# One decoder layer on one core: the last mLSTM head's second split in another buffer, value tiles in another order of PSUM banks, and the right-side loads of the cross-attention queries held behind another load

## The chip, the cores and the metric

The kernel runs on one core of one Trainium2 chip. The metric is the device time of one execution in microseconds (us), lower is better. The program uses the five engines of the core: PE (matrix multiply), DVE (vector), ACT (activation functions and scaled copies), POOL (GpSimd) and SP, which here issues all the DMAs. Each engine runs its own queue of instructions in order.

## The reference, cut to what matters

The layer works on `SEQ = 1024` tokens of width 1024 and 256 memory tokens, all in float32.

```python
h = rmsnorm(x, ln1[l]); z = h @ w_in[l]
mh = mlstm_chunkwise(mq, mk, mv, ig, lf)              # 4 heads of 128
mh = mh * lax.rsqrt(jnp.mean(mh * mh, axis=-1, keepdims=True) + EPS)
ml_out = (mh * ml_norm).reshape(B, S, ML_W) * jax.nn.sigmoid(ml_o)
fx_out = forgetting_attention(fq, fk, fv, flf)        # 8 heads of 64
x = x + jnp.concatenate([ml_out, fx_out], axis=-1) @ w_out[l]
x = x + cross_attention(rmsnorm(x, ln_x[l]), rmsnorm(mem, ln_mem[l]), w_xq[l], w_xkv[l], w_xo[l])
u = jax.nn.relu(rmsnorm(x, ln2[l]) @ w_ff1[l])
x = x + (u * u) @ w_ff2[l]
return rmsnorm(x, ln_f)
```

## The kernel before, in words

Activations are kept with the features on the 128 partitions and the tokens along the free dimension, in two halves of 512 tokens (`hf` 0 and 1). Nearly every product is made of three matmuls on a value that is cut into a high and a low part (`mm3`, L186 to L188): low weight by high input, high by low, high by high. `split` makes the two parts: one ACT copy for the high part (L134, or L137 with a scale) and one DVE subtraction for the low part (L135 or L138).

The stages that the change touches, in order of time:

- **mLSTM head, closing part** (`ml_head`, L568 to L633). For each half it loads a row of factors `fb` into the buffer `r_a` (one buffer; L253 for the first half, L625 for the second), multiplies the head's output by norm and gate (DVE L628, L629), splits it (ACT L137, DVE L138) and stores the parts to the DRAM tensor `mix` (L632, L633). The high part `yh` stands in `r_y`, of which there is one buffer; the low part stays in `r_f`. `r_d` has two buffers.
- **Values of the forgetting attention** (`token_major(a["w_fv"], fv_sink, ...)`, L1092). Sixteen tiles of 24 matmuls (128x256 outputs). Each tile takes a PSUM bank from `mm()`, which goes round the list `banks`: "mm", "tp", "m2", "tp" (the profile calls m2 "m"). "tp" has two banks, "mm" and "m2" one each. Tile 0 takes "mm" and tile 15 "tp": 64 tiles have been drawn since the count `turn` was last set to 0. `fv_sink` splits each tile (ACT L137, DVE L138 with `rcol`) into `r_b`, `r_p` or `r_c` in turn and stores it. The planner mixes these matmuls with the first 13 slots of the attention.
- **Slots of the forgetting attention** (`slot`, L1026). One slot has one score part (`sc` banks, PE L734 and L735), its maximum (DVE L741 or L744), its exponential (ACT L756) and, from the 14th slot on, one value step: transposes into a "tp" bank (PE L782), a split into `r_d` and `r_e` (ACT L134, DVE L135; every third step uses a `w4` buffer), and the product (PE L801). Inside the slots the order of each compute engine is fixed by hand (`in_order`).
- **Second part of the output projection** (`full_sink`, L1122 to L1134). Sixteen tiles, in the order half 0 features 0 to 3, half 1 features 0 to 3, half 0 features 4 to 7, half 1 features 4 to 7. Each loads a piece of `x1d` (L1125), adds it (DVE L1126), stores it back (L1127), and adds its square to a sum (ACT L222, POOL L226). `mix_done` keeps the store of half 1, feature 5, the 14th of the sixteen.
- **Queries of the cross-attention.** `query_whole(hd)` makes the queries of half 0 for one of four heads as plain products: two weight loads from `w_xq` (L174, two `wr` buffers), two products, one in "mm" and one in "m2" (one bank each), each split into `r_b` and `r_c`, or `r_p` and `r_a` or `r_y`. `right_side(hd)` (L1168 to L1188) prepares, for the queries of half 1, which are made by a seven-product scheme, one quarter of the right sides: it loads two pieces of `x1d` into the two `r_f` buffers, here called x (feature `hd`) and y (feature 4 + `hd`) (L1176), scales each (ACT L1177), and makes sums and differences on POOL (`sub`, L1339), each split into an "act" buffer. In code order: cut 11 (from x), cut 21 and 22 (from y), difference and cut t1 (from x alone), difference and cut t2 (t1 and y), difference and cut t3 (x and y), a last difference. The loop calls `query_whole(hd)`, `right_side(hd)` and `cross_head(hd, 0, ...)` for the four heads; the last loads keys and values (L1276, L1277).

What sets the order outside the slots is a planner (`schedule_with_timeline_sim`): it plays the program through with modelled durations, and gives each engine, SP too, the instructions in the order in which they become ready there, earlier code first. Data dependencies and free buffers are waited for. `tc.issue_after(i)` adds that the loads in its body stand behind instruction i in the queue that issues them; it waits for no completion.

Of the kernel before, what the change touches and what calls it, by code (L numbers as in the profile page):

```python
# [10 lines left out]
F32R = mybir.dt.float32r  # L11
# [6 lines left out]
P = 128  # L18
# [5 lines left out]
MLH = 4  # L24
# [20 lines left out]
def hybrid_layer(ctx: ExitStack, tc: tile.TileContext, a: dict, out: bass.AP):  # L45
# [9 lines left out]
    def name(tag):  # L55
        count[0] += 1
        return f"{tag}_{count[0]}"

    def sb(tag, shape, bufs, dt=F32):
        return pool.tile(shape, dt, tag=tag, name=name(tag), bufs=bufs)  # L60
# [18 lines left out]
    def w2(tag, n=512, dt=F32, p=P):  # L79
        return sb("r_" + tag, [P, 512], BUFS[tag], dt)[:p, :n]  # L80
# [6 lines left out]
    def ps_tile(tag):  # L87
        return psum.tile([P, 512], F32, tag=tag, name=name(tag), bufs=PBUFS[tag])

    def sc():  # L90
        return ps_tile("sc")
# [4 lines left out]
    def ov_():  # L96
        return ps_tile("ov")

    turn = [0]
    banks = ["mm", "tp", "m2", "tp"]  # L100
# [10 lines left out]
    load = nc.sync.dma_start  # L111
# [57 lines left out]
    def weights(src, n=1024):  # L169
        return weight_parts(weight_load(src, n))  # L170

    def weight_load(src, n=1024):
        raw = sb("wr", [P, 1024], 2)[:, :n]
        load(raw, src)  # L174
        return raw

    def weight_parts(raw):
        n = raw.shape[1]
        hi = sb("wh", [P, 1024], 3, F32R)[:, :n]
        lo = sb("wl", [P, 1024], 3, F32R)[:, :n]  # L180
        split(hi, lo, raw)
        return hi, lo
# [7 lines left out]
    def both(pair, f):  # L190
        return f(pair[0]), f(pair[1])
# [66 lines left out]
    def proj(w, x, tiles, kn=KT, order=None, into=None):  # L258

        wv = both(w, lambda t: t.rearrange("p (k c) -> p k c", k=kn))  # L260
        for half, n in order or [(hf, n) for n in range(tiles) for hf in range(2)]:
            ps = mm() if into is None else into
            for k in range(kn):
                mm3(ps, both(wv, lambda t: t[:, k, n * P : (n + 1) * P]), both(x[half], lambda t: t[:, k]), k == 0, k == kn - 1)
            yield n, half, ps
# [163 lines left out]
    ps = ov_()  # L429
# [58 lines left out]
    def token_major(w_src, sink, cs=(0, 1), between={}):  # L488

        for c in cs:  # L490
            ws = [both(weights(w_src[c, i]), lambda t: t.rearrange("p (k c) -> p k c", k=4)) for i in range(2)]
            for t in range(8):
                if t in between:
                    between[t]()
                hf, tt = divmod(t, 4)
                ps = mm()[:, 0:256]
                for k in range(KT):
                    x = both(h[hf], lambda z: z[:, k, tt * P : (tt + 1) * P])
                    mm3(ps, x, both(ws[k // 4], lambda z: z[:, k % 4]), k == 0, k == KT - 1)
                sink(t, c, ps)  # L500
# [67 lines left out]
    def ml_head(hd, q, k, og, num1, den1):  # L568
        fac = col("fac", 8)
        nums = []  # L570
        dens = col("dens", 8)
        sqs = col("sqs", 8)
        for hf in range(2):
            nmb = w2("a")
            load(nmb, rows[hd : hd + 1, hf * TH : hf * TH + TH].broadcast_to([P, TH]))
            num = ov_()
            acc = den1 if hf else w2("b")
            last = 4 * hf + 3
            for j in range(4 * hf, last + 1):
                d0 = j - 4 * hf  # L580
                c0 = min(d0 * P, 256)
                sp = sc()
                ks = both(k, lambda z: z[:, j * P : (j + 1) * P])
                mm3(sp[:, c0:], ks, both(q, lambda z: z[:, hf * TH + c0 : hf * TH + TH]), True, True)
                wt = acc if j == 0 else w2("c")
                s.activation(wt[:, c0:], nmb[:, c0:], AF.Exp, bias=gcol[:, j, hd : hd + 1])
                n_ = d0 * P + P - c0
                g.affine_select(out=wt[:, c0 : c0 + n_], in_=wt[:, c0 : c0 + n_], pattern=[[1, n_]], compare_op=ALU.is_ge, fill=0.0, base=c0 - d0 * P, channel_multiplier=-1)
                v.scalar_tensor_tensor(out=wt[:, c0:], in0=sp[:, c0:], scalar=float(P) ** -0.5, in1=wt[:, c0:], op0=ALU.mult, op1=ALU.mult)
                wh, wl = w2("d", dt=F32R), w2("e", dt=F32R)  # L590
                split(wh[:, c0:], wl[:, c0:], wt[:, c0:])
                if j:
                    g.tensor_tensor(out=acc[:, c0:], in0=wt[:, c0:], in1=acc[:, c0:], op=ALU.add)
                vj = mv_of(hd, j)
                mm3(num[:, c0:], (vj[:, :P], vj[:, P:]), (wh[:, c0:], wl[:, c0:]), d0 == 0, j == last)
            sq = w2("c")
            if hf:
                nsb = num1
                v.tensor_tensor(out=nsb, in0=num, in1=nsb, op=ALU.add)
                s.activation(sq, nsb, AF.Square)  # L600
            else:
                nsb = w2("f")
                s.activation(nsb, num, AF.Copy)
                s.activation(sq, num, AF.Square)
            ps = sc()
            sum_cols(ps[:, 0:4], acc, 4)
            sum_cols(ps[:, 4:8], sq, 4)
            s.activation(dens[:, 4 * hf : 4 * hf + 4], ps[:, 0:4], AF.Abs)
            v.tensor_copy(sqs[:, 4 * hf : 4 * hf + 4], ps[:, 4:8])
            nums.append(nsb)  # L610
        v.tensor_tensor(out=dens, in0=dens, in1=emc[:, :, hd], op=ALU.max)
        rd = col("rd", 8)
        v.reciprocal(rd, dens)
        v.tensor_tensor(out=sqs, in0=sqs, in1=rd, op=ALU.mult)
        v.tensor_tensor(out=sqs, in0=sqs, in1=rd, op=ALU.mult)
        rsqrt_cols(fac, sqs, 1.0 / P, 8)
        v.tensor_tensor(out=fac, in0=fac, in1=rd, op=ALU.mult)
        yield
        for hf in range(2):
            fb = w2("a")  # L620
            at = facd[hd : hd + 1]
            if hf == 0:
                to_row(fb, fac, 8, at, sc)
            else:
                load(fb, at[:, TH:].broadcast_to([P, TH]))  # L625
            yield
            y = nums[hf]
            v.scalar_tensor_tensor(out=y, in0=y, scalar=vec[:, VEC["ml_norm"] + hd : VEC["ml_norm"] + hd + 1], in1=fb, op0=ALU.mult, op1=ALU.mult)  # L628
            v.scalar_tensor_tensor(out=y, in0=og[:, hf * TH : hf * TH + TH], scalar=1.0, in1=y, op0=ALU.add, op1=ALU.mult)  # L629
            yh, yl = w2("y", dt=F32R), y.bitcast(F32R)  # L630
            split(yh, yl, y, 0.5)
            load(mix[hf, 0, :, hd], yh.bitcast(F32))  # L632
            load(mix[hf, 1, :, hd], yl.bitcast(F32))  # L633
# [454 lines left out]
    for i in range(LEAD_):  # L1088
        slot(False, 0)
        if i in (1, 11):  # L1090
            next(closing, None)
    token_major(a["w_fv"], fv_sink, between={4: lambda: next(closing, None)})  # L1092
    hm = act().rearrange("p a b -> p (a b)").rearrange("p (e k c) -> p e k c", e=2, k=KT)
    load(hm.bitcast(F32), hmd)
# [20 lines left out]
    h2 = act(), act()  # L1115
    x1_accs = [w2("b"), w2("b")]
    mix_done = []
# [21 lines left out]
    for n0 in (0, 4):  # L1139
        ws = [weights(a["w_out_b"][n0 // 2 + i], 6 * P) for i in range(2)]  # L1140
        for hf in range(2):
            for n in range(n0, n0 + 4):
                w = both(ws[n // 2 % 2], lambda t: t.rearrange("p (k c) -> p k c", k=3)[:, :, n % 2 * P : n % 2 * P + P])
                ps = mm()
# [23 lines left out]
    def right_side(k):  # L1168
        if not fourth:
            for c in (("11", "21"), ("t1", "t2"), ("22", "t3")):  # L1170
                right_room(*c)
            fourth.append(w4((P, 4, 256)))
        x, y = w2("f"), w2("f")
        for t, n in ((x, k), (y, 4 + k)):
            with tc.issue_after(mix_done[0].ins):
                load(t, x1d[1, :, n])  # L1176
            s.activation(t, t, AF.Copy, scale=ln_x(n))  # L1177
        x1, x2, y1, y2 = (t[:, e * 256 : e * 256 + 256] for t in (x, y) for e in range(2))
        cut_right("11", k, x1)
        cut_right("21", k, y1)  # L1180
        cut_right("22", k, y2)
        sub(x1, x2, x1, g)
        cut_right("t1", k, x1)
        sub(x1, y2, x1, g)
        cut_right("t2", k, x1)
        sub(x2, y2, x2, g)
        cut_right("t3", k, x2)
        sub(fourth[0][:, k], y1, x1, g)  # L1188

    def q_room(kk):  # L1190
        return [rotate(*tags).bitcast(F32R) for tags in ((("b",), ("c",)), (("p",), ("a", "y")))[kk]]

    def query_whole(hd):
        q = []
        for kk in range(2):
            t = q_room(kk)
            for _, _, ps in proj(weights(a["w_xq"][2 * hd + kk]), [h2], 1, order=[(0, 0)], into=ps_tile(("mm", "m2")[kk])):
                split(*t, ps, 1.0 / 16.0)
            q.append(t)
        return q  # L1200
# [488 lines left out]
    for at, (b, m) in enumerate(steps):  # L1689
# [16 lines left out]
        for i, of, y, op in ((1, 1, x22, ALU.add), (5, 5, x22, ALU.add), (7, 7, x22, ALU.add), (6, 6, x22, ALU.add), (2, 1, x11, ALU.add), (4, 5, x21, ALU.subtract), (3, 7, x12, ALU.subtract)):  # L1706
            if of == i:
                held[of] = bank()
            ps = held[of]
# [138 lines left out]
```

## Time and profile before

| | us |
|---|---|
| median of 3 runs | 1512.09 (1512.07 to 1512.88) |
| the profiled execution's own time | 1510.96 |
| its span, first to last instruction | 1509.2 |
| PE busy in the span | 1493.0 (99%) |
| DVE, ACT, POOL busy | 1122.7, 757.7, 528.7 |
| mean granted PE clock | 0.997 |

The profiled execution's own time is 1.76 us above its span and 1.13 us below the median. With PE busy for 99% of the span, what can be won or lost without changing the matmuls is the idle time of PE and the time in which its clock is lower. A profile line names an instruction group by source line, engine, operation and tiles (`r_f<-x1d` is a load of `x1d` into an `r_f` buffer).

### The profile page before, as it was taken

Reading aid. Unit: us, or ns where it says so; the run is one execution under the profiler, and the core shown is the slowest. Engines: PE = TensorE matmul, PEld = TensorE weight load, DVE = VectorE, ACT = ScalarE, POOL = GpSimd, SP = SyncE. Lnnn points to the kernel's source line nnn. Section 1 sums busy time; section 2 is a strip of 40 time slices with the busy share of each in tenths; the row PEclk is TensorE's granted clock in tenths of the full one; section 3 lists DMA queues with packets and bytes.
Section 4 is the critical chain, followed back from the end, with each engine's and each line's share of the span. In section 5 each row is a group of like instructions: output and inputs, shape, how many; then the busy total and the mean of one; then the engine's idle time right before and its main releaser. Section 6 shows DMA issues by size and latency. Waiting matters only on the chain.

```text
span 1509.2 us, 22358 instructions
## 1 busy us (share of the span) xinstructions
PE 1493.0 (99%) x7806; PEld 1263.7 (84%) x7806; DVE 1122.7 (74%) x1803; ACT 757.7 (50%) x1440; POOL 528.7 (35%) x545
## 2 busy tenths in 40 slices
PE   9999999999999999999999999999999999999997
PEld 9988888889899888788988878888888888888887
DVE  7766676664788875667767899989996678787765
ACT  7324343334688764566654467566664521122134
POOL 1003030414365441623300044454544365553312
PEclk9999999999999999999999999999999999999999
DMA  6322333435777877853354447676678677776623
GB/s 243 115 79 95 98 108 126 132 129 153 247 261 256 284 248 246 271 169 126 128 182 159 147 155 279 235 261 248 217 273 292 264 279 279 279 272 251 247 88 112
DMA packets 124276, 303.04 MB, mean 201 GB/s; under 512 B 13810, under 2 KB 28460, under 8 KB 117252
## 3 DMA queue, kind: packets, MB, share of 16 engines
q1 hardware_dynamic: 124164, 301.62, 57.3%
q8 instruction: 61, 1.00, 0.3%
q14 instruction: 51, 0.42, 0.1%
HBM read 202.75 MB, written 98.82 MB: 200 GB/s over the span
## 4 chain that ended last, share of the span: by engine, by line
PE 90%; DMA 4%; DVE 3%; ACT 1%; issue 1%; POOL 1%; POOLq 0%; DVEq 0%; SPq 0%; ACTq 0%
PE tp L186 8%; PE tp L187 8%; PE tp L188 8%; PE sc L186 6%; PE sc L188 6%; PE sc L187 6%; PE mm L186 5%; PE m L188 5%; PE m L186 5%; PE m L187 5%; PE mm L188 5%; PE mm L187 5%; PE ov L801 2%; PE ov L186 2%; PE ov L187 2%; PE ov L188 2%
## 5 line engine op out<-in xcount | busy, mean ns | idle before, releaser
L186 PE MATMUL tp<-act,wl 128*128 128x512 f32 (+1 forms) x440 | 172.6, 392 | 0.0
L187 PE MATMUL tp<-act,wh 128*128 128x512 f32 (+1 forms) x440 | 172.1, 391 | 0.0
L188 PE MATMUL tp<-act,wh 128*128 128x512 f32 (+1 forms) x440 | 171.8, 392 | 0.0
L135 DVE TENSOR_TENSOR wl<-wr,wh 128x1024 fp32r<-128x1024 f32 (+2 forms) x99 | 131.4, 1327 | 27.0 <-ACT wh L134 26.7
L134 ACT ACTIVATE wh<-wr 128x1024 fp32r<-128x1024 f32 (+2 forms) x99 | 99.8, 1008 | 85.7 <-PE tp L188 32.7
L186 PE MATMUL mm<-act,wl 128*128 128x512 f32 (+1 forms) x332 | 124.8, 376 | 2.6 <-DVE r_c L138 2.1
L188 PE MATMUL mm<-act,wh 128*128 128x512 f32 (+1 forms) x332 | 124.1, 374 | 0.0
L187 PE MATMUL mm<-act,wh 128*128 128x512 f32 (+1 forms) x332 | 123.8, 373 | 0.0
L186 PE MATMUL m<-act,wl 128*128 128x512 f32 (+1 forms) x308 | 113.8, 369 | 0.6 <-DVE wl L135 0.6
L188 PE MATMUL m<-act,wh 128*128 128x512 f32 (+1 forms) x308 | 113.8, 369 | 0.0
L187 PE MATMUL m<-act,wh 128*128 128x512 f32 (+1 forms) x308 | 113.7, 369 | 0.0
L188 PE MATMUL sc<-act,wh 128*128 128x512 f32 (+1 forms) x280 | 105.6, 377 | 0.0
L187 PE MATMUL sc<-act,wh 128*128 128x512 f32 (+1 forms) x280 | 105.6, 377 | 0.0
L186 PE MATMUL sc<-act,wl 128*128 128x512 f32 (+1 forms) x280 | 105.6, 377 | 0.0
L1612 POOL TENSOR_TENSOR z<-wr 128x256 f32<-128x256 f32 x56 | 52.9, 966 | 131.8 <-DMA wr<-w_ff2q 126.7
L188 PEld LDWEIGHTS tp<-act,wh 128*128 128x128 f32 x440 | 82.7, 188 | 19.0
L186 PEld LDWEIGHTS tp<-act,wl 128*128 128x128 f32 x440 | 82.7, 188 | 18.5
L187 PEld LDWEIGHTS tp<-act,wh 128*128 128x128 f32 x440 | 82.7, 188 | 18.2
L134 ACT ACTIVATE wh<-z 128x1024 fp32r<-128x1024 f32 (+1 forms) x54 | 55.5, 1027 | 81.8 <-POOL z L1612 62.3
L135 DVE TENSOR_TENSOR wl<-z,wh 128x1024 fp32r<-128x1024 f32 (+1 forms) x54 | 77.7, 1439 | 11.4 <-ACT wh L134 11.4
L134 ACT ACTIVATE w<-wr 128x768 fp32r<-128x768 f32 (+3 forms) x35 | 28.0, 801 | 107.4 <-PE tp L186 33.0
L186 PEld LDWEIGHTS mm<-act,wl 128*128 128x128 f32 x332 | 62.7, 189 | 14.2 <-DVE r_c L138 2.6
(734 smaller groups left out, 4387.2 us busy)
## 6 DMA issues: line engine op xcount, KB each, us to landing
act<-right SPq DMA_DIRECT2D x49, 1024.0 KB
right<-w SPq DMA_DIRECT2D x56, 256.0 KB
wr<-w_ff2q SPq DMA_DIRECT2D x28, 512.0 KB
right<-r_d SPq DMA_DIRECT2D x49, 256.0 KB
right<-r_e SPq DMA_DIRECT2D x49, 256.0 KB
act<-fqk SPq DMA_DIRECT2D x48, 256.0 KB
wr<-w_in SPq DMA_DIRECT2D x20, 512.0 KB
wr<-w_ff SPq DMA_DIRECT2D x20, 512.0 KB
```

Source lines behind the costliest of these rows:

```text
L134: s.activation(hi, src, AF.Copy)
L135: return v.tensor_tensor(out=lo, in0=src, in1=hi.bitcast(F32), op=ALU.subtract)
L186: nc.tensor.matmul(ps, w[1], x[0], start=first, stop=False, skip_group_check=more)
L187: nc.tensor.matmul(ps, w[0], x[1], start=False, stop=False, skip_group_check=more)
L188: nc.tensor.matmul(ps, w[0], x[0], start=False, stop=last, skip_group_check=more)
L801: nc.tensor.matmul(self.ov[:, c0:], self.fv[:, self.j], t[:, c0:], start=self.j == 0 and t is self.p[1], stop=self.last and t is self.p[0])
L1612: g.tensor_tensor(out=o, in0=x, in1=y, op=op)
```

## The change

```diff
@@ ml_head, second loop over hf
-            yh, yl = w2("y", dt=F32R), y.bitcast(F32R)
+            yh, yl = w2("d" if hf and hd == MLH - 1 else "y", dt=F32R), y.bitcast(F32R)
@@ after the 13 leading slots
+    banks[:] = ["tp", "tp", "mm", "m2"]
+    turn[0] = 0
     token_major(a["w_fv"], fv_sink, between={4: lambda: next(closing, None)})
@@ right_side
-            with tc.issue_after(mix_done[0].ins):
+            with tc.issue_after(query_raw[0].ins):
                 load(t, x1d[1, :, n])
@@ queries of half 0
+    query_raw = []
+
     def query_whole(hd):
...
-            for _, _, ps in proj(weights(a["w_xq"][2 * hd + kk]), [h2], 1, order=[(0, 0)], into=ps_tile(("mm", "m2")[kk])):
+            raw = sb("wr", [P, 1024], 2)
+            query_raw[:] = [load(raw, a["w_xq"][2 * hd + kk])]
+            for _, _, ps in proj(weight_parts(raw), [h2], 1, order=[(0, 0)], into=ps_tile(("mm", "m2")[kk])):
```

There are three edits. First, the high part of the second half of the last mLSTM head stands in `r_d` in place of `r_y`. Second, the sixteen value tiles take their banks in the order "tp", "tp", "mm", "m2", beginning at "tp", so that the last two are in "mm" and "m2". Third, the loads of `right_side(hd)` stand behind the second weight load of `query_whole(hd)` in SP's queue, and no longer behind the 14th store of the output projection; the weight loads themselves are the same two instructions as before, written out so that the second can be named. `cross_head` keeps its edge to `mix_done`.

## The prediction

> **What bounds the kernel now.** I read the page first, then the waits of PE, then the stretches round its longest wait, then the chain of waits and the queues of POOL and ACT there. The page says that PE is all but full:
>
> ```profile
> PE 1493.0 (99%) x7806; PEld 1263.7 (84%) x7806; DVE 1122.7 (74%) x1803; ACT 757.7 (50%) x1440; POOL 528.7 (35%) x545
> ```
>
> So only what stops or slows PE counts. Of its waits in the whole span, by who ended them (us in total, times, longest), the longest is
>
> ```profile
> PE mm L186 <- DVE r_c L138: 2.1, 1, 2.1
> ```
>
> and these stand where the value tiles meet the attention's slots:
>
> ```profile
> PE sc L734 <- ACT act L756: 1.6, 3, 1.1
> PE sc L734 <- ACT w L756: 0.4, 1, 0.4
> PE tp L782 <- DVE r_b L138: 0.4, 1, 0.4
> ```
>
> The first is in the queries of half 0. The table by stretches of 2 us (busy time and count by engine, then granted clock, DMA share, GB/s) shows that it costs more than itself:
>
> ```profile
> 384.00:386.00 2.00, 0.93 (x6) 0.65 (x5) 2.00 (x7) 1.11 (x4) 0.29 (x1) 1.00 1.00 410
> ...
> 640.00:642.00 2.00, 0.26 (x1) 0.26 (x2) 1.73 (x3) 1.98 (x5) 1.52 (x2) 1.00 0.65 262
> 642.00:644.00 2.00, 2.00 (x7) 1.52 (x7) 2.00 (x4) 1.46 (x3) 0.00 (x0) 0.62 0.59 162
> 644.00:646.00 2.00, 2.00 (x8) 1.62 (x7) 1.10 (x2) 1.14 (x2) 0.00 (x0) 0.53 0.97 352
> ```
>
> Behind the wait of 2.1 us the granted clock is 0.62 and then 0.53. That is 2 x 0.38 + 2 x 0.47 = **1.7 us** of work not done. In the first row PE also stands for 1.1 us (0.93 busy of 2.00), and the clock stays at 1.00. So this one place costs 2.1 + 1.7 = 3.8 us, more than 0.2% of the run (3.0 us), which is about what a measurement of this kernel can tell from no change.
>
> How did PE come to wait? The chain of waits (start, duration, what) passes through the loads of the first `right_side`:
>
> ```profile
> 626.28 4.76 DMA x1d<-r_p
> 631.04 0.02 issue
> 631.05 3.82 DMA r_f<-x1d
> ```
>
> Piece y is loaded at 631.05, as soon as the store of that feature, sent at 626.28, has landed; it is there at 634.87. What follows is seen in POOL's queue and then in ACT's (start, duration, line, operation, tiles, and in brackets the idle time before it):
>
> ```profile
> 636.60 1.29 POOL L226 TENSOR_TENSOR r_b<-r_c,r_b 128x512 f32<-128x512 f32 x1 [2.29 <-ACT r_c L222]
> 637.85 0.92 POOL L1339 TENSOR_TENSOR r_f<-r_f 128x256 f32<-128x256 f32 x1
> 638.84 0.87 POOL L1339 TENSOR_TENSOR r_f<-r_f,r_f 128x256 f32<-128x256 f32 x1
> 640.07 0.73 POOL L1339 TENSOR_TENSOR r_f<-r_f,r_f 128x256 f32<-128x256 f32 x1 [0.36 <-DVE act L135]
> ```
> ```profile
> 639.74 0.42 ACT L134 ACTIVATE act<-r_f 128x256 fp32r<-128x256 f32 x1 [0.53 <-POOL r_f L1339]
> 640.18 0.60 ACT L137 ACTIVATE r_b<-mm 128x512 fp32r<-128x512 f32 x1
> 640.68 1.05 ACT L134 ACTIVATE wh<-wr 128x1024 fp32r<-128x1024 f32 x1
> 641.62 0.41 ACT L134 ACTIVATE act<-r_f 128x256 fp32r<-128x256 f32 x1
> ```
>
> On POOL: a square sum of the output projection, then the differences for t1, t2 and t3. On ACT: the cut of t2, the split of the first query out of "mm", a cut of weights, the cut of t3. The split frees the only "mm" bank, which PE's next product needs. It was due a whole product (24 matmuls) earlier, and stands in ACT's queue behind the cut of t2, which waits for POOL.
>
> **The change part by part.** *Loads behind the weight load.* No instruction comes or goes; the loads of `right_side` may be issued sooner. SP's queue says how much:
>
> ```profile
> 606.69 0.90 SPq L1127 DMA_DIRECT2D x1d<-r_e  x2
> ...
> 611.08 0.42 SPq L1127 DMA_DIRECT2D x1d<-r_d  x1
> 611.59 0.38 SPq L174 DMA_DIRECT2D wr<-w_xq  x1
> 612.03 0.44 SPq L1127 DMA_DIRECT2D x1d<-r_p  x1
> 616.42 0.80 SPq L1125 DMA_DIRECT2D r_d<-x1d  x2
> ```
> ```profile
> 626.87 0.32 SPq L1127 DMA_DIRECT2D x1d<-r_d  x1
> 627.24 4.13 SPq L1176 DMA_DIRECT2D r_f<-x1d  x2
> ```
>
> The last row holds x and y together; the store at 626.87 is the 14th, and x follows it directly, so the old edge held x. Its data are half 1, feature 0, the fifth store, second in the row at 606.69. The weight load of the new edge is the one at 611.59. So x can go out near 612, some 15 us sooner, and with 3.8 us for a load (row 631.05) to about 5 it lands near 617. Piece y needs the 13th store to land and stays at 631.05. For heads 1 to 3 the order of the code puts the weight loads ahead already; I cost those at nothing.
>
> What leaves the stretch after 634.87 is all that x needs alone: its scaling, the cut of 11, the difference for t1 (0.92) and the cut of t1. They fall into the output projection, where ACT and DVE wait for loads such as that of 616.42. When y is scaled,
>
> ```profile
> 634.90 0.73 ACT L1177 ACTIVATE r_f<-r_f,vec 128x512 f32<-128x512 f32 x1 [0.93 <-DMA r_f<-x1d]
> ```
>
> the difference for t2 can run on POOL at once, from 635.63 to 636.5, ahead of the square sum, whose square ACT makes only behind that scaling. Then POOL has the square sum (1.29, to 637.9) and t3 (0.73, to 638.6). Where does the planner put the query's split now? Before, it let it in between the cuts of t2 and t3. Both are about one difference earlier now, so I expect it behind the cut of t3. The difference ahead of it then ends at 638.6, not at 639.7 (638.84 + 0.87); a cut, the split and DVE's part follow as before. PE's wait goes from 2.1 to **1.0 us**. As that is no longer than the wait at 384, the clock stays up, and the 1.7 us go too: **-1.1 - 1.7 = -2.8 us**. Bounds: -3.8 (the split ahead of all of it) and 0. Next to be late is the split of the second query out of "m2", but that bank isn't asked for until a further product of 24 matmuls is through.
>
> The Trainium skill, "TensorE: Matmul & The Clock Gate", section "What's actually happening", halves the array's clock after an idle window of about 3.4 us, in windows that run freely, and its section "HAM oscillation" makes of it that no idle gap should be longer than that. By this rule a wait of 2.1 us alone would leave the clock up; here it is at 0.53 behind one, so I go by the measurement. By the rule the sum would be -1.1 us.
>
> What could be lost is cover: x's 256 KB go out in this stretch,
>
> ```profile
> 612.00:614.00 2.00, 2.00 (x10) 1.64 (x9) 2.00 (x2) 1.14 (x2) 1.69 (x2) 1.00 0.47 120
> ```
>
> right behind the store (611.08) whose landing lets the load of 616.42 go. At 350 GB/s they are 0.75 us. The DMA share of 0.47 leaves room and the same load is gone from 627.24, so I take 0 and keep +0.75.
>
> *Second split in another room.* ACT's queue at that place:
>
> ```profile
> 390.29 0.63 ACT L137 ACTIVATE r_y<-r_f 128x512 fp32r<-128x512 f32 x1 [1.27 <-DMA mix<-r_y]
> 390.83 0.46 ACT L137 ACTIVATE r_c<-m,rcol 128x256 fp32r<-128x256 f32 x1
> 393.00 0.47 ACT L137 ACTIVATE r_b<-tp,rcol 128x256 fp32r<-128x256 f32 x1 [1.72 <-PE tp L188]
> 393.44 0.60 ACT L134 ACTIVATE r_d<-tp 128x512 fp32r<-128x512 f32 x1
> ...
> 394.78 0.49 ACT L134 ACTIVATE r_d<-tp 128x384 fp32r<-128x384 f32 x1
> ```
>
> The 1.27 us for the first half's store out of `r_y` go. But ACT waits 1.72 us for PE right afterwards, so PE wasn't waiting for it: worth nothing. Moved forward among the exponentials, its 0.63 us may hold up a score, 0 to +0.6. I take 0: value matmuls stand beside them in PE's queue, and if that cover failed the 0.6 would be paid.
>
> *Order of the banks.* The last value tile is in "m2", so the second transposes (0.4 us, waiting for `r_b`) find a free "tp". But the score behind them
>
> ```profile
> 394.76 0.44 PE L734 MATMUL sc<-act 128*128 128x384 f32 x1 [0.16 <-ACT act L756]
> ```
>
> waits for an exponential that isn't touched, and would wait 0.4 us longer. From -0.6 (0.4 and 0.16) to +0.6 (as much lost at the first tiles, while the last projections still hold "tp"); I take 0, the reading of the row. The count before the reset is 64, whole rounds, so later banks don't shift.
>
> The sum is -2.8 us. The profiled execution goes from 1510.96 to 1508.2; the median, 1.1 us above it, from 1512.09 to **1509.3**.
>
> **The rivals.** *No wait at all:* the split comes right behind the cut of t2 (636.5 + 0.42), before PE has ended the second product. For it: it came behind t2 until now. Against it: t2 was later then. -3.8 us, 1508.3.
>
> *Nothing gained:* the loads keep their order after all, or POOL takes the square sum first and then t2 and t3 (637.9 + 0.9 + 0.9 = 639.7, as now). 0 us, 1512.1. Against it: y's scaling comes before that square on ACT.
>
> *The clock by the rule:* the low clock has another cause than the wait and stays; only 1.1 us go, 1511.0. Against it: the rows at 384 and 642. The rule is that of the Trainium skill, "TensorE: Matmul & The Clock Gate", section "HAM oscillation".
>
> *Slower, through `r_d`:* its two buffers are also those of the first two value steps, cut at 393.44 and 394.78. The store out of `r_y` was issued here:
>
> ```profile
> 381.15 0.32 SPq L632 DMA_DIRECT2D mix<-r_y  x1
> ```
>
> and was waited for until 390.29, 9.1 us. If the new split keeps its place on ACT (389.0, without the wait), its store goes out at 389.7 and lands at 398.8, and the second value step's cut stands 4.0 us with all exponentials behind it; PE has little else then. That is over the 2.1 us behind which the clock fell: 4.0 + 1.7 - 2.8 = +2.9 us, 1515.0, and 1517.8 if the queries gain nothing. It decides from a store sent after 394.78 - 9.1 = 385.7. Against it: DVE's gate product for that half,
>
> ```profile
> 384.77 0.69 DVE L629 SCALAR_TENSOR_TENSOR r_f<-w,r_f 128x512 f32<-128x512 f32 x1
> ```
>
> ends at 385.46, so the split can follow at once and the store go out at 386.1, only 0.4 us behind that point.
>
> **How the numbers follow.** Forecast 1509.3: 0.33 (own range 1508.5 to 1510.3). No wait: 0.18. Nothing gained: 0.18. Clock by the rule: 0.06. Slower, through the room, or x's load with the chain that it delays, or an order that I don't foresee: 0.25. Faster by over 0.2% (below 1509.07): the second case and over a third of the first, 0.30. Slower (above 1515.1): two thirds of the last, 0.18 with rounding. Within: 0.52. The range goes from 1507.5 (no wait, and 0.6 from the banks with a little spread) to 1516.0, which leaves out the upper part of the slower case.
>
> **What would show it.** Right: SP issues the first `r_f<-x1d` just behind the second `w_xq` load, near 612, and the second near 631; PE's wait for `r_c` at 640 is about 1 us; no stretch there has a clock under 0.9; ACT no longer waits for `mix<-r_y`. Wrong: that wait is still 2 us, PE or ACT waits for `r_d`, or x and y still go out together behind the 14th store.

## The result, and the profile after

The changed kernel takes 1514.59 us (median of 22 runs, 1512.68 to 1516.56), the kernel before 1512.51 us beside it (22 runs, 1510.31 to 1514.91). The ratio is 1.0013, with a 95% interval of 1.0007 to 1.0019: it is **slower by about 2 us** (1.1 to 2.9), where 2.8 us less had been forecast. The time lies inside the stated range and inside the 0.2% either way, on the other side of the forecast.

The profiled execution of the changed kernel took 1513.8 us, with a span of 1512.1 us. The page, busy time by engine:

```profile
PE 1493.4 (99%) x7806; PEld 1263.0 (84%) x7806; DVE 1121.7 (74%) x1803; ACT 758.1 (50%) x1440; POOL 531.5 (35%) x545
```

PE does the same work in the same time (1493.0 before), so again only its idle time and its clock count. The waits of PE between 600 and 700 us (who ended them; us in total, times, longest):

```profile
PE m L186 <- DVE r_d L1128: 1.5, 1, 1.5
PE ov L186 <- ACT r_d L134: 1.2, 1, 1.2
PE ov L234 <- POOL r_b L226: 1.0, 1, 1.0
PE sc L186 <- ACT z L1299: 0.3, 1, 0.3
```

The wait of 2.1 us for `r_c` is gone, as the change intends, and four others stand in its place, 4.0 us together. The stretches of 2 us show where they lie and what the clock does (busy time and count of PE, PEld, DVE, ACT, POOL, then granted clock, DMA share, GB/s):

```profile
622.00:624.00 2.00, 1.44 (x7) 0.83 (x5) 0.47 (x1) 1.84 (x4) 0.00 (x0) 1.00 0.96 371
624.00:626.00 2.00, 1.07 (x5) 0.88 (x6) 2.00 (x5) 1.93 (x5) 1.83 (x2) 1.00 0.83 318
...
630.00:632.00 2.00, 1.21 (x6) 0.64 (x4) 1.70 (x3) 0.48 (x1) 2.00 (x1) 1.00 0.74 281
632.00:634.00 2.00, 1.83 (x11) 1.71 (x12) 0.58 (x1) 1.25 (x3) 1.92 (x3) 0.90 0.56 108
634.00:636.00 2.00, 2.00 (x6) 1.56 (x5) 1.00 (x1) 1.62 (x4) 1.92 (x2) 0.50 0.69 244
636.00:638.00 2.00, 2.00 (x8) 1.55 (x8) 2.00 (x4) 1.73 (x6) 1.93 (x3) 0.74 0.78 304
```

PE stands for 1.5 us round 624 and for about 1 us round 631, and then the clock falls: 2 x (0.10 + 0.50 + 0.26) = 1.7 us of work lost, as much as before, only 9 us sooner (from 633.6 us, against 642.5).

What PE waits for is found by going backwards through the queues. It waits for DVE to free bank "m" (`r_d`, L1128). DVE's queue in the changed kernel (start, duration, line, operation, tiles, idle time before it):

```profile
617.19 0.68 DVE L1128 TENSOR_TENSOR r_e<-mm,r_e 128x512 f32<-128x512 f32 x1
623.53 0.75 DVE L138 SCALAR_TENSOR_TENSOR act<-r_e,vec,act 128x512 fp32r<-128x512 f32 x1 [5.66 <-ACT act L137]
624.20 0.68 DVE L1128 TENSOR_TENSOR r_d<-m,r_d 128x512 f32<-128x512 f32 x1
```

DVE stood for 5.66 us because ACT had not made the high part of `r_e`. The addition that frees the bank stands behind that, in order. ACT's queue:

```profile
614.83 0.73 ACT L137 ACTIVATE act<-r_p,vec 128x512 fp32r<-128x512 f32 x1 [1.03 <-DVE r_p L1128]
622.16 0.72 ACT L1179 ACTIVATE r_f<-r_f,vec 128x512 f32<-128x512 f32 x1 [6.60 <-DMA r_f<-x1d]
622.79 0.71 ACT L137 ACTIVATE act<-r_e,vec 128x512 fp32r<-128x512 f32 x1
```

ACT had nothing to do for 6.60 us, though `r_e` was ready at 617.87 (617.19 + 0.68): the next instruction in its queue was the scaling of x (L1179), and x had not come. In the kernel before, ACT waited at this place for `r_e` alone, and DVE's addition into `r_d` ran as soon as its own load was there:

```profile
617.23 0.72 ACT L137 ACTIVATE act<-r_e,vec 128x512 fp32r<-128x512 f32 x1 [2.34 <-DVE r_e L1126]
```
```profile
621.69 0.69 DVE L1126 TENSOR_TENSOR r_d<-m,r_d 128x512 f32<-128x512 f32 x1 [2.95 <-DMA r_d<-x1d]
```

So 2.3 of the 6.60 us are not new, and 4.3 us (617.87 to 622.16) are the wait for x. POOL, which adds the squares that ACT makes, stood too, and then was behind:

```profile
613.42 3.29 POOL L226 TENSOR_TENSOR r_b<-r_c,r_b 128x512 f32<-128x512 f32 x2 [0.30 <-ACT r_c L222]
624.09 2.88 POOL L226 TENSOR_TENSOR r_b<-r_c,r_b 128x512 f32<-128x512 f32 x2 [7.38 <-ACT r_c L222]
...
628.08 7.99 POOL L226 TENSOR_TENSOR r_b<-r_c,r_b 128x512 f32<-128x512 f32 x5
```

Those squares are what PE waits for at 631 (`ov L234 <- POOL r_b`). And why was x late? SP's queue:

```profile
612.08 0.38 SPq L1202 DMA_DIRECT2D wr<-w_xq  x1
612.58 0.39 SPq L1129 DMA_DIRECT2D x1d<-r_p  x1
617.09 0.32 SPq L1127 DMA_DIRECT2D r_d<-x1d  x1
617.46 0.42 SPq L1178 DMA_DIRECT2D r_f<-x1d  x1
...
631.88 0.32 SPq L1178 DMA_DIRECT2D r_f<-x1d  x1
```

The edge does what it says: x no longer stands behind the 14th store, and x and y are issued apart. But x's load (617.46) did not go out behind the weight load of 612.08; the planner put it behind the next `r_d` load (617.09), and that one waits in SP's queue until the store that empties `r_d` has landed. The chain of waits of the changed kernel (start, duration, what) shows that landing:

```profile
611.56 5.47 DMA x1d<-r_d
...
617.46 0.42 SPq L1178
```

So x arrived at about 622.1, not near 617, 4.7 us after its issue. The wait of 1.2 us for `r_d` at 668 is the same thing once more: ACT waits for a later head's piece, with the split that PE needs behind it. By ACT's queue so is that of 0.3 us for `z`, which ACT makes at 659.33 behind two scalings that stood 2.47 and 0.71 us for their loads.

```profile
667.54 0.72 ACT L1179 ACTIVATE r_f<-r_f,vec 128x512 f32<-128x512 f32 x1 [1.36 <-DMA r_f<-x1d]
...
668.62 1.07 ACT L134 ACTIVATE r_d<-tp 128x512 fp32r<-128x512 f32 x2
```

### The profile page after: what moved, and what is told of

The parts are those of the page before. It is cut to its first block, busy times and chain, and to the rows that moved or that the text cites. A ratio compares the mean times of both kernels' runs of the same rounds, so it can differ in the third digit from the quotient of the medians.

```text
span 1512.1 us, 22367 instructions
## 1 busy us (share of the span) xinstructions
PE 1493.4 (99%) x7806; PEld 1263.0 (84%) x7806; DVE 1121.7 (74%) x1803; ACT 758.1 (50%) x1440; POOL 531.5 (35%) x545
## 4 chain that ended last, share of the span: by engine, by line
PE 90%; DMA 4%; DVE 2%; ACT 1%; issue 1%; POOL 1%; SPq 0%; POOLq 0%; DVEq 0%; ACTq 0%
PE tp L186 8%; PE tp L187 8%; PE tp L188 8%; PE sc L186 7%; PE sc L188 6%; PE sc L187 6%; PE m L186 5%; PE m L187 5%; PE m L188 5%; PE mm L186 5%; PE mm L188 5%; PE mm L187 5%; PE ov L186 2%; PE ov L801 2%; PE ov L187 2%; PE ov L188 2%
## 5 line engine op out<-in xcount | busy, mean ns | idle before, releaser
L188 PEld LDWEIGHTS mm<-act,wh 128*128 128x128 f32 x332 | 62.8, 189 | 11.6
```

The lines of the kernel that those rows point to most:

```text
L188: nc.tensor.matmul(ps, w[0], x[0], start=False, stop=last, skip_group_check=more)
```

## The experiments

**Theory (the scaling):** the third edit alone costs the time, because it puts x's scaling early into ACT's queue, where it waits for x and holds up what is behind it. **Rival A (the chance and the rooms):** the first two edits gain or lose something by themselves, and the sum only looks like the third. **Rival B (the load):** it is x's transfer itself, in a stretch full of stores and loads, and not the place of its scaling. All ratios are to the kernel before, run on the same chip beside the experiment.

### Edit by edit: room, banks, edge

`room` has the first edit alone, `banks` the second, `edge` the third:

```diff
# room
+            yh, yl = w2("d" if hf and hd == MLH - 1 else "y", dt=F32R), y.bitcast(F32R)
# banks
+    banks[:] = ["tp", "tp", "mm", "m2"]
+    turn[0] = 0
# edge
+            with tc.issue_after(query_raw[0].ins):
```

Expected of `room`:

> The first edit alone (the second split of the last mLSTM head in r_d). Theory A (the loss of the change is the early load of x: ACT stands for it, in order): this edit has no part in the loss; ACT no longer waits for mix<-r_y near 390, PE's waits between 380 and 400 (2.4 us before) shrink by at most 0.5 us, the queries near 640 are as before with PE's wait of 2.1 us; time -0.5 to 0 us. Rival R (the room r_d holds up the value steps): ACT or PE waits for r_d near 394, +0.5 us or more.

Expected of `banks`:

> The second edit alone (value tiles in the order tp, tp, mm, m2). Theory A: the gain of about 1.4 us that the changed kernel shows between 374 and 393 us belongs to this edit and the first together; here at most all of it, -1.4 to 0 us, queries as before. Rival B (the gain there is chance of one execution): the profile has PE waits of 2 us or more between 380 and 400, 0 us.

Expected of `edge`:

> The third edit alone (loads of right_side behind the second weight load). Theory A: x goes out near 617, lands near 622, ACT stands some 6 us for it, PE waits near 623 (1.5 us) and 631 (1 us), the clock falls once; +1.5 to +3.5 us. Rival B (the three edits lose only together, or the whole difference lies in the first 20 us): within 0.5 us of before.

Measured: `room` 1511.92 against 1511.73 us, ratio 1.0004 (0.9995 to 1.0012); `banks` 1511.67, 0.9999 (0.9990 to 1.0008); `edge` 1513.63, **1.0017 (1.0009 to 1.0026)**. The waits of PE in `edge`, between 600 and 700 us:

```profile
PE sc L186 <- ACT z L1297: 1.4, 1, 1.4
PE ov L186 <- ACT r_d L134: 1.1, 1, 1.1
PE ov L234 <- POOL r_b L226: 1.0, 1, 1.0
PE m L186 <- DVE r_d L1126: 0.9, 1, 0.9
```

and the place in ACT's queue of `edge`:

```profile
621.33 0.72 ACT L1177 ACTIVATE r_f<-r_f,vec 128x512 f32<-128x512 f32 x1 [6.62 <-DMA r_f<-x1d]
```

The third edit alone makes the same four waits, in other sizes, with the same 6.6 us of ACT ahead of them, and costs 1.9 us (1.4 to 3.9). The other two are at nothing.

### The first two together: room_banks

Both lines of `room` and `banks`, without the third edit.

> The first two edits without the third. Theory A: faster than before by the 1.4 us between 374 and 393, the wait of 2.1 us near 640 with its low clock stays: -1.4 us. Rival B (the first two edits slow something too): 0 us or slower.

Measured: 1511.80 against 1511.73 us, ratio 1.0000 (0.9991 to 1.0009). Rival A falls. The first profile of the changed kernel had passed the value tiles 1.3 us sooner than before (95.19 us from the start of matmul 1650 to that of matmul 2300, against 96.46), and `banks` takes 95.22 there; but this kernel takes 96.22, a second profile of the changed kernel 96.44 and a third 98.38. What looked like a gain of the banks is no more than what single executions differ by.

### The scaling of x held back: scale_late

The changed kernel, with the scaling of x and y put behind the square of the 14th tile in ACT's queue. The loads keep their places.

```diff
         if hf == 1 and n == KT - 3:
             mix_done.append(done)
+            mix_act.append(<the last ACT instruction>)
...
-            s.activation(t, t, AF.Copy, scale=ln_x(n))
+            with tc.issue_after(mix_act[0]):
+                s.activation(t, t, AF.Copy, scale=ln_x(n))
```

> The changed kernel with one more edge: x (and y) of right_side are still loaded early, but their scaling on ACT stands behind the square of the 14th tile of the output projection. Theory A (the loss is ACT standing in order for x): the waits of PE near 623 and 631 us go, ACT has no idle stretch of 6 us there; time within 0.7 us of before, 1.5 to 2.5 us under the changed kernel. Rival D (the early load itself, by its traffic and its place in SP's queue, delays the loads of the projection): the waits stay, +1.5 us or more.

Measured: 1513.09 against 1511.94 us, ratio 1.0008 (0.9999 to 1.0017), 1.2 us above the kernel before where 0.7 at most had been expected. x's load in SP's queue, and ACT's queue:

```profile
617.64 0.42 SPq L1180 DMA_DIRECT2D r_f<-x1d  x1
```
```profile
618.09 0.72 ACT L137 ACTIVATE act<-r_e,vec 128x512 fp32r<-128x512 f32 x1 [2.35 <-DVE r_e L1129]
...
627.80 0.71 ACT L1182 ACTIVATE r_f<-r_f,vec 128x512 f32<-128x512 f32 x1
...
639.77 0.42 ACT L134 ACTIVATE act<-r_f 128x256 fp32r<-128x256 f32 x1 [2.19 <-POOL r_f L1348]
640.21 0.60 ACT L137 ACTIVATE r_b<-mm 128x512 fp32r<-128x512 f32 x1
```

The split of `r_e` runs at 618.09 instead of 622.79, and the waits of PE near 624 and 631 are gone, although x's load goes out at the same place as in the changed kernel (617.64, there 617.46). So they come from the place of the scaling, and rival B falls for those two waits. And the first query's split now comes right behind the cut of t3, the order that the prediction expected, and with the wait that it worked out for it:

```profile
PE sc L186 <- DVE r_y L138: 1.0, 1, 1.0
PE mm L186 <- DVE r_c L138: 1.0, 1, 1.0
PE sc L186 <- DVE r_a L138: 0.6, 1, 0.6
```

1.0 us for `r_c`, as forecast. But new waits for `r_y` and `r_a` stand later among the queries, and the time didn't come down to that of the kernel before.

### The same again: scale_late_2, with after_2 beside it

> The changed kernel with x's and y's scaling behind the square of the 14th tile, again, beside the changed kernel. Theory A: the waits near 623 and 631 us are gone again and the time is 0.5 to 1.5 us under the changed kernel's; what is left above before (0 to 1.2 us) lies in the later queries, where the first profile had two waits of 1.0 and 0.6 us. Rival D (the early load costs by itself): no difference from the changed kernel.

> The changed kernel again, on the same chip as the next two. Theory A: +1.1 to +2.9 us against before; waits of PE near 623 and 631 us of 0.8 us or more each, ACT standing some 6 us for x.

Measured: `scale_late_2` 1513.14 against 1511.78 us, ratio 1.0012 (1.0003 to 1.0021); the changed kernel again, `after_2`, 1514.59, ratio 1.0016 (1.0007 to 1.0025). The changed kernel's loss is there again. `scale_late_2` is 1.45 us under it by the medians, 0.6 by the means, and the two intervals overlap: how much of the loss the scaling's place gives back is not settled by these runs.

### The split ahead of y's scaling: split_ahead

If ACT's order is what decides, the gain that was looked for must be had without any earlier load. This kernel has the first two edits and the old edge for the loads, and y's scaling behind the first query's split:

```diff
                 split(*t, ps, 1.0 / 16.0)
+                if hd == 0 and kk == 0:
+                    query_act.append(<the last ACT instruction>)
...
-            s.activation(t, t, AF.Copy, scale=ln_x(n))
+            with tc.issue_after(query_act[0]) if t is y else ExitStack():
+                s.activation(t, t, AF.Copy, scale=ln_x(n))
```

> The first two edits, the old edge to the 14th store, and the scaling of y on ACT behind the split of the first query. Theory W (PE's wait near 640 is that split standing behind the cuts that need y): the wait of 1.9 to 2.1 us goes and with it the clock drop where there was one; -1.9 to -3.8 us. Rival N (the cuts that now come later are late for the next product or head, the wait comes back elsewhere among the queries): -0.5 us or nothing.

Measured: **1509.36** against 1511.94 us, ratio **0.9988 (0.9979 to 0.9996)**. The split of the first query in ACT's queue of `split_ahead`:

```profile
635.53 0.60 ACT L137 ACTIVATE r_b<-mm 128x512 fp32r<-128x512 f32 x1
```

It runs 4.65 us sooner than before (640.18), and PE doesn't wait near 640 at all. Some of it comes back later:

```profile
PE sc L186 <- DVE r_c L138: 1.9, 2, 1.3
```

The profiled execution (1511.71 us) is the longest of the kernel's 11 runs. It shows where the wait went, but not the whole gain: its stretch from 590 to 740 us is only 0.8 us better than the mean of the old edge (table further below).

### Both: split_ahead_early, and again

All three edits, x's scaling behind the 14th square as in `scale_late`, y's behind the first split as in `split_ahead`.

> All three edits, x's scaling behind the square of the 14th tile, y's scaling behind the first query's split. Theory W: as split_ahead, -1.9 to -3.8 us, and perhaps 0.5 us more since the difference for t1 has been made before y lands. Rival N: -0.5 us or nothing.

> As the kernel before it, with y's scaling also behind the first query's split, again. Theory W: PE has no wait over 0.5 us between 600 and 690 us, -1 to -3 us against before, and 2 us or more under the changed kernel.

Measured: 1510.01 against 1511.94 us, ratio 0.9990 (0.9981 to 0.9999), and the second time 1509.91 against 1511.78, 0.9985 (0.9976 to 0.9995). Both kernels, with the earlier loads and without, are about 2 us faster than the kernel before, and `split_ahead_early` is 4.7 us faster than the changed kernel measured beside it (1509.91 against 1514.59). The longest wait between 600 and 700 us in the second,

```profile
PE sc L186 <- DVE r_c L138: 1.2, 2, 0.8
```

is 0.8 us, over the 0.5 that had been expected at most. The earlier loads add nothing that can be measured to `split_ahead`: the intervals lie on each other.

### One more profile of each: before_again, after_again

> The kernel before once more, for a second profile of the same program. If the waits of PE in the first 20 us (none above 0.3 us before, 1.7 us in the changed kernel) and the shares of the stretch from 330 to 400 us come from one execution and not from the edits, they differ here from the first profile by up to 1.5 and 1 us; the wait near 640 is 1.8 to 2.3 us, with the clock drop if it is over 2 us.

> The changed kernel once more. Theory A: ACT again stands some 6 us for x near 617 to 622, PE waits near 623 and 631 (together 1.8 us or more); the first 20 us differ from the first profile by up to 1.5 us.

Each is one execution: 1514.36 us for the kernel before and 1514.47 for the changed one, beside a run of the kernel before of 1513.24. As times they say nothing; their traces do. In `before_again` the wait for `r_c` is longer than in the first profile, and longer than the 2.3 us expected at most, and yet the clock holds:

```profile
PE mm L186 <- DVE r_c L138: 3.0, 1, 3.0
```
```profile
640.00:642.00 2.00, 1.03 (x5) 0.50 (x3) 1.87 (x4) 0.42 (x1) 1.92 (x3) 1.00 1.00 352
642.00:644.00 2.00, 0.00 (x0) 0.00 (x0) 1.80 (x3) 1.91 (x4) 1.56 (x3) 1.00 0.92 371
644.00:646.00 2.00, 1.94 (x8) 1.61 (x9) 1.92 (x4) 1.79 (x4) 0.00 (x0) 1.00 0.47 126
```

In `room`, behind a wait of 2.3 us, it falls as in the first profile:

```profile
642.00:644.00 2.00, 1.32 (x4) 1.08 (x5) 1.92 (x4) 2.00 (x4) 0.62 (x1) 0.78 0.12 41
644.00:646.00 2.00, 2.00 (x6) 1.51 (x6) 2.00 (x3) 0.93 (x2) 0.00 (x0) 0.50 1.00 322
```

In `after_again` the waits of 1.3 and 1.0 us at 624 and 631 are there, and the clock falls behind them as in the first profile.

### The profiles side by side

From the table of stretches of every profile, 590 to 740 us: the idle time of PE, and the work lost to a lower clock (length of the stretch times one minus the granted clock), in us.

| kernel | old edge: idle + clock | kernel | new edge: idle + clock |
|---|---|---|---|
| before | 2.6 + 1.7 | edge | 4.4 + 0 |
| before_again | 5.0 + 0 | after | 4.0 + 1.7 |
| room | 2.9 + 1.7 | after_again | 4.0 + 1.7 |
| banks | 3.4 + 0 | after_2 | 3.7 + 1.7 |
| room_banks | 3.2 + 0 | | |
| mean | 4.1 | mean | 5.3 |

`scale_late` has 2.3 and 3.3 there, `split_ahead` 3.3, `split_ahead_early` 1.5 and 2.4, all without a fall of the clock. For `split_ahead_early` that is 2.6 and 1.7 us less than the mean of the old edge, about the 1.9 us of its times. The new edge costs 1.2 us in this stretch by these means, of the 1.9 to 2.8 us between the medians (1.9 for `edge`, 2.1 and 2.8 for the changed kernel). 1.2 us is just inside two of the three intervals (from 1.1 us) and just under the third (`edge`, from 1.4). The rest has no place in the profiles: single executions differ by as much elsewhere. From the first matmul to matmul 100 it is 14.96 us in before and 15.96 in `before_again`, the same program, and 16.64 in `banks`.

For `scale_late` the two ways don't agree: 1.3 us less than the old edge's mean in this stretch by its profiles, 1.2 to 1.4 us more by its times. 0.6 us of that is the wait for `r_a`, which lies behind this stretch: PE stands for 0.63 and 0.65 us between 740 and 800 us in its two profiles, and not at all there in any other. The rest stays open.

## Why the prediction was wrong, point by point

**The step that failed** is the one in which x's scaling, the cut of 11 and the first difference "fall into the output projection, where ACT and DVE wait for loads such as that of 616.42". It took the idle time of ACT for room. ACT does wait there, but for loads that its own queue needs next; and an instruction that is put between them brings its own load with it. The prediction had x issued near 612, landing near 617; it was issued at 617.46, behind a load that waits for a store, and landed at 622.1. ACT stood 6.6 us ahead of its scaling, 4.3 of them for x alone, and DVE 5.7 and POOL 7.4 behind ACT. The term taken as 0 is 1.5 + 1.0 us of PE waits in the first profile (1.3 + 1.0, 1.0 + 1.0 and 0.9 + 1.0 in the others), and with the two waits of the same kind later (1.2 and 0.3) it is more than the whole gain. That the time still lies inside the stated range is luck as far as the sum goes: its upper part was priced by the case of `r_d`, which cost nothing.

**x's transfer,** kept at +0.75 as a bound, was not the cause of the two waits: in `scale_late` it goes out at the same place and they are gone. Whether it has a part in the 1.2 to 1.4 us that `scale_late` keeps is not shown; against it stands `split_ahead_early`, which loads x as early and is within 0.7 us of `split_ahead`. What counted was the time at which x came against the place of its first reader. The rival of the slower side named "x's load with the chain that it delays" beside the room, as a thing of 25%; the chain is this one, but its place and price weren't worked out, and that price was the one to work out.

**The shorter wait at 640** was right in order and in size, once x's scaling is out of the way: 1.0 us in both profiles of `scale_late`. In the changed kernel it is 0, since PE comes to that point later, behind the waits at 624 and 631.

**The 1.7 us of the clock** were taken as the price of that one wait. They aren't. The clock fell behind waits of 2.1 us (before) and 2.3 (`room`), but not behind 1.9 (`banks`), 3.0 (`before_again`), or two of 0.9 and 1.0 (`edge`); and it fell in all three profiles of the changed kernel behind pairs of 1.0 to 1.5 and 1.0 us. So the row at 384, which stood at 1.1 us without a fall, carried no threshold, and the 1.7 us were to be taken as a chance: two of the five profiles with the old edge have it, three of the four with the new one.

The traces also show on what this chance hangs. In each of the five profiles the low clock lasts 3.41 us at 0.50 (before: 642.46 to 645.88), and within a trace the changes of the clock lie whole steps of that length apart: in before the clock comes back at 645.88 and falls once more at 1502.62, at the end of the program, 856.74 us or 251 steps of 3.413 us later. Take the step that ends where the clock falls. It has 2.1 us without a matmul in before and 2.3 in `room`. In the changed kernel it goes from 630.20 to 633.61 and has 1.0 us without a matmul, and 0.9 us in which PE makes eight products of a single column:

```profile
632.17 1.05 PE L234 MATMUL ov<-ones,r_b 128*128 128x1 f32 x8 [0.96 <-POOL r_b L226]
```

The 3.0 us of `before_again` lie across two steps, 1.5 us in each, and in `edge` the wait of 1.0 us and those eight products fall into different steps. So in these profiles it isn't the length of a wait that decides, but how much of it falls into one step; the border lies near 1.9 us (1.87 in `banks`, which doesn't fall, 1.87 and 1.88 in the changed kernel, which does). Where the steps lie differs from execution to execution, so a forecast can only give a chance. This is read from the traces; no run was made to test it.

The Trainium skill, "TensorE: Matmul & The Clock Gate", section "What's actually happening", says that the window of activity runs freely and that where a transition comes depends on where in it the work begins; these traces agree with that, with steps of 3.41 us, and the same kernel falls in one execution (2.1 us) and not in another (3.0 us). Its length of about 3.4 us as the idle time needed does not agree: 2.1 us were enough, and the measurement decides.

**Edits one and two at nothing** was right (1.0004, 0.9999, and 1.0000 together). The wait of ACT for the store out of `r_y` is gone, as was said, and nothing was waiting for it. The slower case through `r_d` didn't come, although its condition was met: ACT and SP of the changed kernel show the split, its store, and the two cuts into `r_d`:

```profile
385.98 0.63 ACT L137 ACTIVATE r_d<-r_f 128x512 fp32r<-128x512 f32 x1
...
393.62 0.60 ACT L134 ACTIVATE r_d<-tp 128x512 fp32r<-128x512 f32 x1
...
394.97 0.49 ACT L134 ACTIVATE r_d<-tp 128x384 fp32r<-128x384 f32 x1
```
```profile
386.64 0.32 SPq L632 DMA_DIRECT2D mix<-r_d  x1
```

The store was sent at 386.64, past the point of 385.7, and yet neither cut waits for it. The 9.1 us taken for its landing were too many here: it is through by 394.97, 8.3 us later, or sooner.

**"For heads 1 to 3 the order of the code puts the weight loads ahead already"** held for the loads' edge but not for the order that follows: the later scalings move too, and one of them holds up the split for PE at 668. In the changed kernel it stands at 667.54, ahead of that split (668.62); in before it comes at 669.83, behind it (663.51). The wait is there in all four profiles of the table with the new edge (1.2 us in the first profile, 1.1, 1.2 and 1.1 in the others) and in none with the old edge.

## What to carry to other kernels

Idle time of an engine that works its queue in order is no room for an instruction with a load of its own: look for what is queued behind the new instruction, and compare its load's landing, behind every wait ahead of it in the issuing queue, with the time at which the next instruction would have been ready. Move a load early if you like, but hold its first reader back by hand to where the data is sure to be there. And when a product waits for a split, the direct cure is to put the split ahead of the work that doesn't matter yet (here 2 us), not to bring that work's data sooner and hope that the order follows.

## What the runs showed that was not expected

- The granted clock falls to 0.50 behind one execution's wait of 2.1 us and stays at 1.00 behind another's of 3.0 us of the same kernel; when it falls, it stays down for 3.41 us, and the cost was 1.7 us in each of the five profiles that have it.
- A store of 256 KB took 5.47 us to land at 611.56, and x's load 4.7 us from its issue, against the 3.8 us of the load that the prediction went by.
- 6.6 us of ACT standing, with DVE and POOL behind it, cost PE only 1.5 + 1.0 us at that place: it ran on with what had been prepared until it asked for bank "m".
